# A squared-ReLU MLP as one level of Strassen's scheme, with sums of the up weights made in DRAM

## The chip, the cores and the metric

The kernel runs on one core of a Trainium2 chip. The core has TensorE (PE, with its weight loads listed as PEld), VectorE (DVE), ScalarE (ACT), GpSimd (POOL) and SyncE (SP), each with an instruction queue of its own, and DMA queues that are fed by SP, ACT and POOL. The metric is the device time of one execution in microseconds (us); smaller is better. A profile is one execution recorded by the hardware profiler, and its times count from the start of its span.

## The reference

One decoder layer on x of 512 tokens by 1024. All weights are float32.

```
h = rmsnorm(x, norm_mix_g)
q, k, v, xr, gr, g_attn, g_rnn = split(h @ w_in)            # 1024 x 7168
attn = diff_attention(q, k, v, ...)                         # 8 heads, two softmaxes each, T5 bias, causal
rnn  = gelu(gr) * RG_LRU(causal_conv4(xr))
x = x + (sigmoid(g_attn) * (attn @ w_proj_attn) + sigmoid(g_rnn) * (rnn @ w_proj_rnn)) @ w_out
h2 = rmsnorm(x, norm_mlp_g)
x = x + square(relu(h2 @ w_up)) @ w_down                    # 1024 x 4096, 4096 x 1024
```

The change concerns the last two lines, which are called the MLP here.

## The kernel before

Activations lie transposed, features on the 128 partitions and the 512 tokens along a row. Every float32 product is made of float32r matmuls: `split` (line 129) writes a high part (a cast by ACT) and a low part (source less high part, by DVE) of each operand, and `mm3` (line 124) adds three matmuls into one PSUM bank: high by high, high by low, low by high. So one product of 128 by 128 weights with 512 tokens is three matmuls of 512 columns, recorded as lines 125, 126 and 127. All calls of DVE, ACT and POOL go through one helper that keeps them in program order (recorded as line 66).

Weights come in units of 128 x 1024 float32 (512 KB): four blocks of 128 in the contraction by 256 outputs. The class `Weights` (line 81) loads a unit on SP into `wraw` (two buffers), casts it to `whi` on ACT and subtracts to `wlo` on DVE (four buffers each); `ahead` and `raws` say how many units are cast and loaded before their use. `cols_proj` (line 137) takes units in order and issues for each 24 matmuls of 512 columns into two banks.

The order of work is that of the program text, with generators that interleave stages:

- the input norm and the first gates (0 to about 45 us);
- QKV projections of four head pairs, and attention in 39 steps of which each holds parts of one or more of 32 (head, row block) softmaxes (function `attention`, which keeps a table of what is done at which step). Between the parts of a step, `fill_in` issues pieces of the next pair's projection. The QK norm takes its power on POOL (`rstd_of`, line 203), and DVE applies it two pieces later. POOL also writes and reads back a small table in DRAM for the norm behind attention (lines 579 and 583);
- the recurrent branch in four chunks, interleaved with the remaining gates and the attention projection (`tick`, line 787);
- the recurrent projection (`y_rnn`), then w_out in four blocks (`merged`, line 835), where the residual goes into x2, and x2 scaled by the norm's gain is split into h2T. The sum of squares for the second norm is collected on POOL;
- the MLP (lines 866 to 912) in two chunks of 2048 hidden features. A chunk has eight `cols_proj` over h2T, drained by `relu2` (ReLU and square on ACT, then split), and four over the chunk's 16 hidden blocks, drained by `down`, which multiplies by the second norm's 1/(mean square) and adds to x2 (DVE). The norm can wait because ReLU squared turns a factor on the input into its square on the output. The last block of the last chunk is done in three parts, two of them 256 tokens wide, so that the output leaves early.

Matmuls of 256 columns with one weight load each occur at two places: in the QKV projection, where the activations are the stationary operand, and in the two last parts of the down projection.

## Time and profile before

| | |
|---|---|
| median of 3 runs | 896.83 us (894.88 to 896.98) |
| the profiled execution | 897.49 us, span 895.6 us |
| instructions | 11845, of which 4704 matmuls and 4704 weight loads |
| HBM read, written | 87.89 MB, 4.76 MB |
| mean DMA rate | 101 GB/s |

A row of the timeline is: start in us, duration in us, engine, line, operation, what it writes and reads, shape, and in brackets the idle time before it with what ended it. A row of the groups by line is: line, engine, operation, output and inputs, shape, count, then the busy time of the group and the mean duration of one in ns, then the idle time of the engine just before them and what ended it. A row of a windows view is: the stretch, its length, then busy time and count for each engine asked for (PE alone, or PE, PEld, DVE, ACT and POOL in that order), the granted TensorE clock, the busy share of the DMA engines and GB/s. A row of the DMA queues is: packets, megabytes, and the time of the packets as a share of 16 engines' span; one of the DMA issues: count, KB each, median us to landing. In the list of waits the numbers are total us, times, and the longest. Matmuls overlap, so that the duration of one is longer than its share of the stream.

### The profile page before, as it was taken

Reading aid. Unit: us, or ns where it says so; the run is one execution under the profiler, and the core shown is the slowest. Engines: PE = TensorE matmul, PEld = TensorE weight load, DVE = VectorE, ACT = ScalarE, POOL = GpSimd, SP = SyncE. Lnnn points to the kernel's source line nnn. Section 1 sums busy time; section 2 is a strip of 40 time slices with the busy share of each in tenths; the row PEclk is TensorE's granted clock in tenths of the full one; section 3 lists DMA queues with packets and bytes.
Section 4 is the critical chain, followed back from the end, with each engine's and each line's share of the span. In section 5 each row is a group of like instructions: output and inputs, shape, how many; then the busy total and the mean of one; then the engine's idle time right before and its main releaser. Section 6 shows DMA issues by size and latency. Waiting matters only on the chain.

```text
span 895.6 us, 11845 instructions
## 1 busy us (share of the span) xinstructions
PE 888.7 (99%) x4704; PEld 751.7 (84%) x4704; DVE 497.3 (56%) x874; ACT 397.1 (44%) x643; POOL 63.1 (7%) x64
## 2 busy tenths in 40 slices
PE   9999999999999999999999999999999999999998
PEld 7899999999888777888878888888888888888887
DVE  6765688877865256787677554433233333333331
ACT  6444355455545337657733344555312235552110
POOL 0021212222000000000000031000000000000000
PEclk9999999999999999999999999999999999999999
DMA  6348222221312332332133533233332232223320
GB/s 204 130 135 249 76 59 75 81 61 59 106 60 83 95 131 69 106 107 93 54 111 95 191 110 102 68 123 103 101 98 94 94 94 94 94 94 105 122 103 25
DMA packets 31048, 90.80 MB, mean 101 GB/s; under 512 B 3712, under 2 KB 6728, under 8 KB 30992
## 3 DMA queue, kind: packets, MB, share of 16 engines
q1 hardware_dynamic: 30096, 87.93, 30.5%
q0 software_dynamic: 896, 2.11, 1.1%
q8 instruction: 37, 0.61, 0.3%
q14 instruction: 19, 0.16, 0.1%
HBM read 87.89 MB, written 4.76 MB: 103 GB/s over the span
## 4 chain that ended last, share of the span: by engine, by line
PE 92%; DMA 3%; DVE 2%; ACT 2%; issue 1%; SPq 0%; ACTq 0%
PE acc L125 27%; PE acc L127 27%; PE acc L126 27%; PE at L511 2%; DMA wraw<-in_w_in_dram 2%; PE at L125 2%; PE at L126 2%; PE at L127 2%; ACT whi L66 1%; PE at L545 1%; DVE wlo L66 1%; PE at L463 1%; PE at L576 1%; DMA wraw<-in_w_pa_dram 0%; ACT tt L66 0%
## 5 line engine op out<-in xcount | busy, mean ns | idle before, releaser
L66 DVE TENSOR_TENSOR wlo<-wraw,whi 128x1024 fp32r<-128x1024 f32 (+2 forms) x150 | 177.9, 1198 | 170.9 <-ACT whi L66 170.2
L66 ACT CAST whi<-wraw 128x1024 fp32r<-128x1024 f32 (+2 forms) x150 | 149.8, 1011 | 191.3 <-PE acc L126 140.5
L125 PE MATMUL acc<-whi,hT 128*128 128x256 f32 x384 | 111.4, 290 | 0.0
L126 PE MATMUL acc<-wlo,hT 128*128 128x256 f32 x384 | 108.9, 284 | 0.0
L127 PE MATMUL acc<-whi,hT 128*128 128x256 f32 x384 | 108.8, 283 | 0.0
L127 PE MATMUL acc<-h2T,wlo 128*128 128x512 f32 x256 | 100.5, 393 | 0.0
L125 PE MATMUL acc<-h2T,whi 128*128 128x512 f32 x256 | 100.4, 392 | 0.0
L126 PE MATMUL acc<-h2T,whi 128*128 128x512 f32 x256 | 99.7, 389 | 0.0
L125 PE MATMUL acc<-hT,whi 128*128 128x512 f32 x208 | 82.3, 396 | 0.0
L127 PE MATMUL acc<-hT,wlo 128*128 128x512 f32 x208 | 81.5, 392 | 0.5 <-DVE wlo L66 0.5
L126 PE MATMUL acc<-hT,whi 128*128 128x512 f32 x208 | 81.5, 392 | 0.0
L125 PEld LDWEIGHTS acc<-whi,hT 128*128 128x128 f32 x384 | 73.2, 191 | 4.3 <-issue 3.0
L126 PEld LDWEIGHTS acc<-wlo,hT 128*128 128x128 f32 x384 | 73.3, 191 | 0.7 <-issue 0.5
L127 PEld LDWEIGHTS acc<-whi,hT 128*128 128x128 f32 x384 | 73.2, 191 | 0.6 <-issue 0.4
L66 ACT ACTIVATE pe<-pe,nm 128x128 f32<-128x128 f32 (+3 forms) x64 | 35.5, 556 | 65.3 <-DVE nm L66 65.3
L126 PEld LDWEIGHTS acc<-h2T,whi 128*128 128x128 f32 x256 | 48.1, 188 | 10.9
L127 PEld LDWEIGHTS acc<-h2T,wlo 128*128 128x128 f32 x256 | 48.1, 188 | 10.7
L125 PEld LDWEIGHTS acc<-h2T,whi 128*128 128x128 f32 x256 | 48.1, 188 | 10.0
L66 POOL TENSOR_TENSOR rs<-ms,mhalf 128x8 f32<-128x8 f32 (+1 forms) x25 | 39.7, 1589 | 213.9 <-DVE ms L66 213.9
L125 PE MATMUL acc<-up,whi 128*128 128x512 f32 (+1 forms) x136 | 51.7, 380 | 0.0
L127 PE MATMUL acc<-up,wlo 128*128 128x512 f32 (+1 forms) x136 | 51.6, 379 | 0.0
L125 PE MATMUL acc<-upT,whi 128*128 128x512 f32 (+1 forms) x136 | 51.4, 378 | 0.0
(197 smaller groups left out, 1662.5 us busy)
## 6 DMA issues: line engine op xcount, KB each, us to landing
wraw<-in_w_in_dram SPq DMA_DIRECT2D x52, 512.0 KB, 3.4
wraw<-in_w_up_dram SPq DMA_DIRECT2D x32, 512.0 KB, 3.3
wraw<-in_w_dn_dram SPq DMA_DIRECT2D x32, 512.0 KB, 3.3
wraw<-in_w_pa_dram SPq DMA_DIRECT2D x8, 512.0 KB, 4.4
wraw<-in_w_pr_dram SPq DMA_DIRECT2D x8, 512.0 KB, 3.3
wraw<-in_w_o_dram SPq DMA_DIRECT2D x8, 512.0 KB, 4.4
trep<-tdram SPq DMA_DIRECT2D x8, 320.0 KB, 5.0
toep<-trep SPq DMA_DIRECT2D x8, 256.0 KB, 3.9
```

Source lines behind the costliest of these rows:

```text
L66: ins = f(*a, **k)
L125: T.matmul(o, l[0], r[0], start=first, stop=False)
L126: T.matmul(o, l[0], r[1], start=False, stop=False)
L127: T.matmul(o, l[1], r[0], start=False, stop=last)
L463: T.transpose(out=ps[:, t * P:(t + 1) * P], in_=qn[t // 2][:, c0:c0 + P], identity=ident)
L511: T.matmul(lg[c][:, :N], qT[r, x0, i * P:(i + 1) * P], kT[r, y0, :N], start=a == 0, stop=a == 2)
L545: T.transpose(out=tp[:, b * P:(b + 1) * P], in_=st[s][:, b * P:(b + 1) * P], identity=ident)
L576: T.matmul(ps[:, t:t + 1], sq[:, t * P:(t + 1) * P], ones, start=True, stop=True)
```

## The change

The MLP is divided into 16 units: for each of four chunks of 1024 hidden features two up units (512 outputs by 1024 contraction) and two down units (512 outputs by 1024 contraction). A unit is a 2 x 2 by 2 x 2 block product over half outputs, half contraction and half tokens, and is made of seven products M1 to M7 instead of eight. Each product is 8 blocks of weights with 256 tokens, three matmuls each: 24 matmuls of 256 columns. Three PSUM banks (X, Y, Z) serve a unit; several products add into the same bank one after the other.

The seven products need sums and differences:

- of the activations: for the up units from h2 (made once in `merged`, seven forms in `h2s`), for the down units from the squared ReLU (made in `up_out`, with `act_sums` on DVE, seven forms in `us`);
- of the down weights: made in place in the raw buffers by DVE, four additions of 128 x 1024 a unit (`plus_for`);
- of the up weights: made in DRAM. `weight_sums` copies blocks with two transfers a unit on ACT's queue, and adds with three accumulating transfers on POOL's queue. `prep` advances it, by half a transfer for each attention step, then in `tick` and in later stages. SP loads the sums like other weights, with seven loads for an up unit and four for a down unit.

The order of the products, the casts ahead of them (up to four units of weights) and the moments of the deferred ACT and DVE work (`later`, in multiples of `STEP`, counted in planned time) are written out. The first up units are begun with three of four blocks of the contraction. The norm is applied differently: x2 is multiplied by the mean square, and the regions that the last two units write are multiplied by its reciprocal at the end. The squares are added by DVE instead of POOL. The host lays w_up and w_down out in blocks for this.

```diff
-    for ch in range(2):
-        for j in range(8):
-            wb.cols(w_up, 2048 * ch + 256 * j)
-        for j in range(4):
-            wb.cols(w_dn, 256 * j, 16 * ch, 16)
+
+    DU = [(kind, ch, m) for ch in range(4) for kind in ("up", "down") for m in range(2)]
+    UP = [v for v in range(16) if DU[v][0] == "up"]
+    sums13, sums42 = ({v: dp.tile([2, P, 1024], F32, name=f"t{z}{v}", tag=f"t{z}{v}") for v in UP} for z in "ab")
+
+    def blocks(v):
+        kind, ch, m = DU[v]
+        return (w_up if kind == "up" else w_dn)[2 * ch + m].rearrange("a b p c -> (a b) p c")
+
+    def weight_sums():
+        def init(v):
+            A.dma_start(sums13[v], blocks(v)[0:4:3])
+            A.dma_start(sums42[v], blocks(v)[2:4])
+
+        init(UP[0])
+        for n in range(10):
+            if n + 1 < 8:
+                init(UP[n + 1])
+            if n < 8:
+                G.dma_start(sums13[UP[n]], blocks(UP[n])[1:2].broadcast_to([2, P, 1024]), accum_op=ALU.add, max_dma_last_dim=8192)
+                yield
+            if 0 <= n - 1 < 8:
+                G.dma_start(sums42[UP[n - 1]][1], sums13[UP[n - 1]][0], accum_op=ALU.add, max_dma_last_dim=8192)
+                yield
+            if 0 <= n - 2:
+                G.dma_start(sums42[UP[n - 2]][0], sums42[UP[n - 2]][1], accum_op=ALU.add, max_dma_last_dim=8192)
+                yield
+
+    ws_gen, ws_owed = weight_sums(), [0.0]
+
+    def prep(amount):
+        ws_owed[0] += amount
+        while ws_owed[0] >= 1.0:
+            ws_owed[0] -= 1.0
+            next(ws_gen, None)
...
+            prep(0.5)
...
+            prep(0.08 * cost)
...
-        run(y_rnn(mh))
+        mh = hp.tile([P, 2, KT, S], F32R, tag="hT", name="mT")
+        mh = [mh[:, j] for j in range(2)]
+        for _ in y_rnn(mh):
+            prep(0.15)
...
+    FORM = {"M1": 0, "M4": 1, "M2": 2, "M5": 3, "M6": 4, "M7": 5, "M3": 6}
+
+    def hi_part(dst, src):
+        A.copy(dst[:, 0], src)
+
+    def lo_part(dst, src):
+        V.tensor_tensor(out=dst[:, 1], in0=src, in1=dst[:, 0].bitcast(F32), op=ALU.subtract)
+
+    def act_sums(f, fs, which=range(4)):
+        for n in which:
+            a, b = {0: (f[1], f[2]), 1: (fs[:, 0], f[0]), 2: (f[0], f[1]), 3: (f[3], fs[:, 1])}[n]
+            V.tensor_tensor(out=fs[:, n], in0=a, in1=b, op=ALU.add if n == 3 else ALU.subtract)
...
+            f1 = scratch[:, 4 + 2 * (j % 2):6 + 2 * (j % 2), :].rearrange("p a (u s) -> p a u s", u=2)
+            d = h2s[j // 2][:, :, :, j % 2, :]
+            f = f1[:, 0, 1, :], f1[:, 0, 0, :], f1[:, 1, 0, :], f1[:, 1, 1, :]
             for c in range(2):
                 t = 2 * j + c
                 V.tensor_tensor(out=x2[:, t, :], in0=ps[c], in1=x2[:, t, :], op=ALU.add)
-                split(h2T[0][:, t, :], h2T[1][:, t, :], x2[:, t, :], smt[:, C_G2 + t:C_G2 + t + 1])
+                g2 = smt[:, C_G2 + t:C_G2 + t + 1]
+                if c == 0:
+                    for h in range(2):
+                        A.activation(f[h], x2[:, t, 256 * h:256 * h + 256], AF.Copy, scale=g2)
+                else:
+                    A.activation(f1[:, 1, ::-1, :], x2[:, t, :].rearrange("p (h s) -> p h s", h=2), AF.Copy, scale=g2)
+            fs = fin.tile([P, 4, 2, 256], F32, tag="fs", name="h2fs")[:, :, 0, :]
+            for src, dst in ((f[0], d[:, :, 0]), (f1[:, 1], d[:, :, 1:3])):
+                hi_part(dst, src)
+            act_sums(f, fs)
+            for src, dst in ((f[0], d[:, :, 0]), (f1[:, 1], d[:, :, 1:3])):
+                lo_part(dst, src)
+            hi_part(d[:, :, 3:7], fs)
+            lo_part(d[:, :, 3:7], fs)
             for c in range(2):
                 t = 2 * j + c
-                sq = ssq if t == 0 else fin.tile([P, S], F32, tag="relu", name="sq2", bufs=2)
+                sq = ssq if t == 0 else scratch[:, 2 + t % 2, :]
                 A.activation(sq, x2[:, t, :], AF.Square)
                 if t:
-                    G.tensor_tensor(out=ssq, in0=ssq, in1=sq, op=ALU.add)
+                    owing.append(lambda sq=sq: V.tensor_tensor(out=ssq, in0=ssq, in1=sq, op=ALU.add))
...
+    ORD = {"up0": ("M1", "M2", "M6", "M5", "M7", "M3", "M4"), "up1": ("M1", "M5", "M6", "M2a", "M7", "M2b", "M4", "M3"),
+           "down0": ("M1", "M5", "M6", "M2", "M7", "M3", "M4"), "down1": ("M1", "M5", "M6", "M2", "M7", "M3", "M4")}
...
+    steps = []
+    for v, (kind, ch, m) in enumerate(DU):
+        if v == 0:
+            g, r = range(3), range(3, 4)
+            steps += [step(0, "M1", g), step(0, "M2", g), step(0, "M5", g), step(1, "M1", g), step(0, "M1", r), step(0, "M2", r), step(1, "M1", r)]
+            steps += [step(0, p, r if p == "M5" else every) for p in ("M6", "M5", "M7", "M3", "M4")]
+        else:
+            steps += [step(v, p) for p in ORD[kind + str(m)] if (v, p) != (1, "M1")]
...
+    for v, p in ops:
+        up, b = DU[v][0] == "up", blocks(v)
+        if up:
+            need.append(len(loads) + 1)
+            loads.append((v, p, {"M1": b[0], "M2": b[2], "M3": b[3], "M5": sums13[v][0], "M7": sums13[v][1], "M6": sums42[v][1], "M4": sums42[v][0]}[p]))
+        else:
+            for q, n in (("M1", 0), ("T", 1), ("M3", 3), ("M2", 2)):
+                if p == "M1":
+                    loads.append((v, q, b[n]))
+            need.append(None)
...
+    def load():
+        while n_load[0] < len(loads) and n_load[0] < n_free[0] + 4:
+            n = n_load[0]
+            if n < EARLY or len(wb.raw) == len(wb.reqs):
+                v, p, src = loads[n]
+                t = fin.tile([P, 4, 256], F32, tag="rx", name="raw", bufs=2) if n % 4 < 2 else wp.tile([P, 4, 256], F32, tag="wraw", name="raw", bufs=2)
+                nc.sync.dma_start(t, src.rearrange("p (k c) -> p k c", k=4))
+                raw[v, p] = t
+                n_load[0] += 1
+            else:
+                break
+
+    def drop(v, p):
+        dead.add((v, p))
+        while n_free[0] < n_load[0] and loads[n_free[0]][:2] in dead:
+            n_free[0] += 1
...
+    def plus_for(n):
+        if n >= len(ops) or n in added or not loaded(n):
+            return
+        added.add(n)
+        v, p = ops[n]
+        if DU[v][0] == "down":
+            for q, x, y in (("M5", "M1", "T"), ("M6", "M1", "M3"), ("M7", "T", "M3"), ("M4", "M2", "M1")):
+                if q == p:
+                    V.tensor_tensor(out=raw[v, x], in0=raw[v, x], in1=raw[v, y], op=ALU.add)
+                    if q == "M4":
+                        drop(v, "M1")
+
+    def cast_lo():
+        hi, lo, src, (v, p) = half.pop(0)
+        V.tensor_tensor(out=lo, in0=src, in1=hi.bitcast(F32), op=ALU.subtract)
+        lows[0] += 1
+        if DU[v][0] == "up":
+            drop(v, p)
+        elif p in ("M7", "M3", "M4"):
+            drop(v, {"M7": "T", "M3": "M3", "M4": "M2"}[p])
+        load()
+
+    def cast_hi():
+        n = len(units)
+        v, p = ops[n]
+        plus_for(n)
+        slots[0] -= 1
+        src = raw[v, p if DU[v][0] == "up" else {"M5": "M1", "M6": "M1", "M7": "T", "M4": "M2"}.get(p, p)]
+        hi, lo = (wp.tile([P, 4, 256], F32R, tag=t, name=t, bufs=4) for t in ("whi", "wlo"))
+        A.copy(hi, src)
+        units.append((hi, lo))
+        half.append((hi, lo, src, (v, p)))
+
+    def next_lo():
+        if half:
+            cast_lo()
+            plus_for(len(units))
...
+    def up_out(v, p, X, Y, Z):
+        m = DU[v][2]
+        if p == "M1":
+            acts[v] = {"a11": fin.tile([P, 2, 256], F32, tag="a11", name="a11", bufs=2)}
+            us[m] = hp.tile([P, 2, 7, 2, 256], F32R, tag="hT", name="us0") if m == 0 else fin.tile([P, 2, 7, 2, 256], F32R, tag="us", name="us1")
...
+        if p == "M1":
+            A.copy(f0, Y)
+        elif p == "M2":
+            V.tensor_tensor(out=f0, in0=X, in1=f0, op=ALU.add)
+            later(1.1 * STEP if m == 0 else 0.0, lambda: relu2(f0))
+            hl(0, f0, *((1.1, 2.1) if m == 0 else (0.0, 0.6)))
+        elif p == "M6":
+            A.copy(a12, Y)
+        elif p == "M5":
+            A.copy(a22, Z)
+        elif p == "M7":
+            V.tensor_tensor(out=a22, in0=a22, in1=Y, op=ALU.subtract)
+            if m == 1:
+                later(0.0, lambda: relu2(a22))
+                hl(1, a22, 0.6, 1.6)
...
+        elif p == "M4":
+            A.activation(a21, Y, AF.Relu)
+            A.activation(a21, a21, AF.Square)
+            fs = fss[v] = fin.tile([P, 4, 2, 256], F32, tag="fs", name="fs")
+            if m == 0:
+                later(0.0, lambda: relu2(a12))
+                hl(2, a12, 0.5, 1.2)
+                later(1.1 * STEP, lambda: act_sums((f0, a21, a22, a12), fs))
+                hl(slice(3, 7), fs, 2.1, 3.1)
...
+    def down_out(v, p, X, Y, Z):
+        ch, m = DU[v][1:]
+        part = lambda c, h: x2[:, 4 * m + 2 * c:4 * m + 2 * c + 2, 256 * h:256 * h + 256]
+        for q, ps, c, h, op in (("M1", Y, 0, 0, ALU.add), ("M2", X, 0, 0, ALU.add), ("M6", Y, 1, 0, None), ("M5", Z, 1, 1, ALU.add),
+                                ("M7", Y, 1, 1, None), ("M3", Z, 1, 0, ALU.add), ("M4", Y, 0, 1, ALU.add)):
+            if q == p:
+                o = part(c, h)
+                if op is None:
+                    V.tensor_tensor(out=o, in0=o, in1=ps, op=ALU.subtract)
+                else:
+                    V.tensor_tensor(out=o, in0=ps, in1=o, op=op)
+                if ch == 3 and p in ("M2", "M7", "M3", "M4"):
+                    s = slice(256 * h, 256 * h + 256)
+                    V.tensor_tensor(out=o, in0=o, in1=r2[:, s].rearrange("p (o s) -> p o s", o=1).broadcast_to([P, 2, 256]), op=ALU.mult)
+                    t = 4 * m + 2 * c
+                    nc.sync.dma_start(out[t * P:(t + 2) * P, s].rearrange("(u p) s -> p u s", p=P), o)
...
+    def norm2():
+        s2 = fin.tile([P, 2, S], F32R, tag="fs", name="s2")
+        split(s2[:, 0], s2[:, 1], ssq)
         ps = psum("acc")
-        T.matmul(ps, onesr, s2[0], start=True, stop=False)
-        T.matmul(ps, onesr, s2[1], start=False, stop=True)
-        V.tensor_scalar(out=r2, in0=ps, scalar1=1.0 / DM, scalar2=EPS, op0=ALU.mult, op1=ALU.add)
-        V.reciprocal(r2, r2)
+        T.matmul(ps, onesr, s2[:, 0], start=True, stop=False)
+        T.matmul(ps, onesr, s2[:, 1], start=False, stop=True)
+        m = r2
+        V.tensor_scalar(out=m, in0=ps, scalar1=1.0 / DM, scalar2=EPS, op0=ALU.mult, op1=ALU.add)
+        later(32.0, lambda: V.reciprocal(r2, m))
+        for t in range(KT):
+            later(2.0 + 2.5 * t, lambda t=t: V.tensor_tensor(out=x2[:, t, :], in0=x2[:, t, :], in1=m, op=ALU.mult))
...
+    seen, banks = {}, {}
+    for s, (v, p, pairs, halves) in enumerate(steps):
+        kind, ch, m = DU[v]
+        if v not in banks:
+            banks[v] = [psum("acc") for _ in range(3)]
+        X, Y, Z = banks[v]
+        b = {"M2": X, "M5": Z, "M3": Z}.get(p, Y)
+        src = h2s if kind == "up" else us
+        for _ in range(2):
+            if len(units) < number[v, p] + 4 and can_cast():
+                next_lo()
+                cast_hi()
+        while lows[0] <= number[v, p]:
+            if half:
+                next_lo()
+            else:
+                assert can_cast()
+                cast_hi()
+        hi, lo = units[number[v, p]]
+        f = FORM[p]
+        k = seen.get((v, p), 0)
+        seen[v, p] = k + len(pairs) * len(halves)
+        for u in halves:
+            for n, i in enumerate(pairs):
+                a = src[i // 2]
+                for e, (l, r) in enumerate(((hi, 0), (hi, 1), (lo, 0))):
+                    T.matmul(b[:, 256 * u:256 * u + 256], l[:, i, P * u:P * u + P], a[:, r, f, i % 2],
+                             start=p in ("M1", "M2", "M5") and k == n == u == e == 0, stop=i == 3 and e == 2, skip_group_check=True)
+        if seen[v, p] == 8:
+            finish((v, p))
+            (up_out if kind == "up" else down_out)(v, p, two(X), two(Y), two(Z))
+        tick(STEP * len(pairs) * len(halves) / 8)
+        next_lo()
+        if s == 9:
+            norm2()
+        prep(0.4)
...
+    up4 = g["w_up"][0].reshape(4, 2, P, 8, 2, 256).transpose(3, 1, 4, 2, 0, 5).reshape(8, 2, 2, P, 1024)
+    dn4 = g["w_down"][0].reshape(4, 2, 2, 2, P, 2, 2, 256).transpose(0, 5, 2, 6, 4, 1, 3, 7).reshape(8, 2, 2, P, 1024)
```

143 lines of the change are left out of this document (85 added, 58 removed).

## The prediction

> **What bounds the kernel now.** I read the engines' busy table and the chain of waits first, to see which engine sets the end, then the MLP by windows and by timeline, then the groups by line inside the MLP, the waits, and the DMA views.
>
> ```profile
> PE 888.7 (99%) x4704; PEld 751.7 (84%) x4704; DVE 497.3 (56%) x874; ACT 397.1 (44%) x643; POOL 63.1 (7%) x64
> PE 92%; DMA 3%; DVE 2%; ACT 2%; issue 1%; SPq 0%; ACTq 0%
> ```
>
> TensorE has work in 99% of the span and carries 92% of the chain that ended last. A busy TensorE need not be a fast one, so the rate is read from starts. The first two rows are stretches of the MLP (up with the first down; the last down chunks), the next two are the first and the last of 96 matmuls of 256 columns with which the down projection ends.
>
> ```profile
> 540.00:804.00 264.00, 264.00 (x1156) 1.00 0.30 96
> 880.40:891.80 11.40, 11.40 (x97) 1.00 0.10 36
> ...
> 880.45 0.28 PE L125 MATMUL acc<-up,whi 128*128 128x256 f32 x1
> ...
> 891.75 0.28 PE L127 MATMUL acc<-upT,wlo 128*128 128x256 f32 x1
> ```
>
> A 512-column matmul takes 264.0 / 1156 = 0.2284 us of the stream; a 256-column one (891.75 - 880.45) / 95 = 0.119 us. Both run at granted clock 1.00, no gap is left, and the DMA engines are 30% busy. So the MLP, from 540 to 892, is bound by the number of matmul columns and by nothing else. DVE and ACT in the same stretch (540 to 892) have little to do:
>
> ```profile
> L66 DVE TENSOR_TENSOR wlo<-wraw,whi 128x1024 fp32r<-128x1024 f32 x61 | 75.3, 1237 | 99.7 <-ACT whi L66 99.7
> L66 ACT CAST whi<-wraw 128x1024 fp32r<-128x1024 f32 x61 | 64.1, 1051 | 139.9 <-PE acc L126 139.9
> L66 ACT ACTIVATE rsq<-relu 128x512 f32<-128x512 f32 x32 | 20.2, 632 | 1.4 <-PE acc L858 0.4
> L66 ACT ACTIVATE relu<-acc 128x512 f32<-128x512 f32 x32 | 19.0, 595 | 63.8 <-PE acc L127 63.8
> L66 ACT CAST up<-rsq 128x512 fp32r<-128x512 f32 x16 | 9.9, 621 | 0.5
> ```
>
> **The change part by part.** *Matmuls.* Today the MLP issues 1488 matmuls of 512 columns and 96 of 256: 1488 x 0.2284 + 96 x 0.119 = 351.3 us. After it, 16 units of 7 products of 24 matmuls of 256 columns: 2688 x 0.119 = 319.9 us. One eighth of the columns goes, 43.9 us, but a column costs 0.465 ns in a 256-wide matmul instead of 0.446, which gives 12.5 us back: **-31.4 us**. The 96 rows are the operation itself (weights stationary, activations moving, one load for each matmul). The ends of the range are 11.40 / 97 = 0.1175 us (315.9, -35.4) and 6.00 / 49 = 0.1224 (329.0, -22.3) from a stretch of the QKV projection below; I take 0.119, from starts, because the edges of a window cut matmuls and the projection has its operands the other way round.
>
> ```profile
> 57.50:63.50 6.00, 6.00 (x49) 1.00 0.59 197
> ```
>
> [...]
>
> *DVE.* It now holds the sums and differences that the scheme needs. How close its instructions follow one another, from starts:
>
> ```profile
> 39.44 0.74 DVE L66 SCALAR_TENSOR_TENSOR hT<-xT,smt,hT 128x512 fp32r<-128x512 f32 x1
> 40.10 1.22 DVE L66 TENSOR_TENSOR wlo<-wraw,whi 128x1024 fp32r<-128x1024 f32 x1
> 41.24 0.68 DVE L66 TENSOR_TENSOR xT<-xT,rb 128x512 f32<-128x512 f32 x1
> 41.84 0.74 DVE L66 SCALAR_TENSOR_TENSOR hT<-xT,smt,hT 128x512 fp32r<-128x512 f32 x1
> ...
> L66 DVE RECIPROCAL r<-r 128x512 f32<-128x512 f32 x1 | 3.4, 3353 | 0.0
> ```
>
> 1.14 us for 1024 elements and 0.60 for 512, so about 2.2 for 2048. A down unit has 7 low parts (8.0), 4 sums of raw weights (4.6) and 7 drains of PSUM into x2 (4.2): 16.8 us in the 20.0 us that its 7 x 24 matmuls take (84%). An up unit has 7 low parts (8.0), 3 drains (1.8), 4 sums of activations (2.4) and low parts of 7 forms (three of 512, one of 2048: 4.0): 16.2 us (81%). The two units that write the output have four more multiplications each, 19.2 us of 20.0. The norm, moved among them, adds the reciprocal and nine or ten passes of 512, about 9.5 us once. In all 8 x 16.8 + 8 x 16.2 + 4.8 + 9.5 = 278 us of 320: it fits, as the rows of a unit add up, but DVE goes from a spare engine to one that is 87% full. *ACT* in an up unit, by the durations above: 7 high parts (7.4), 4 pairs of relu and square (4.9), 3 copies and 3 casts of 512 (3.7), a cast of 2048 (2.1): 18.1 us of 20.0; in a down unit 7.4.
>
> The stalls that this leaves cannot be seen in the trace of before. The place for them is a down unit's start. Its four raw weights stay until the last product's weights are summed, so the next unit's first load waits for them: a load, a high part and a low part are 3.3 + 1.05 + 1.24 = 5.6 us (the rows of a load stand below), against 2.86 us for a product, with up to four units cast ahead (8.6 us) as cover. From both sides: 0 if the cover holds, 8 x (5.6 - 2.86) = 22 us if it never does. I take 1 us for each of the 8 down units, **+8 us**, nearer the lower end since the cover is longer than the chain; a gain below nothing is excluded, as TensorE has no idle time to give.
>
> *Start and end of the MLP.* The last merged block must be added, scaled, summed and split before its part of the contraction is used. In the queue of DVE that is two additions (1.2), four sums of 256 (1.7 by the row below), low parts of 256, 512 and 1024 (2.2), with ACT's casts between them (2 to 3) and two or three low parts of weights (1.14 each): 9 to 11 us. The first four steps, that use three of the four blocks, cover 72 x 0.119 = 8.6 us. 0 to 4 us, I take **+2**. The same work for the three blocks before, with the adding of the squares that leaves POOL, is about 8 us of DVE for each, beside the 48 x 0.2284 = 11 us of a block's matmuls: nothing, while that cover of 3 us stands. At the end the last addition and multiplication have 512 elements instead of 256, one after the other: **+0.5 us**.
>
> ```profile
> L66 POOL TENSOR_TENSOR ssq<-ssq,sq 128x512 f32<-128x512 f32 x7 | 12.2, 1750 | 42.5 <-ACT sq L66 42.3
> ...
> 892.07 0.42 DVE L66 TENSOR_TENSOR y<-acc,r 128x256 f32<-128x256 f32 x1 [4.82 <-PE acc L127]
> 892.53 0.42 DVE L66 TENSOR_TENSOR x<-y,x 128x256 f32<-128x256 f32 x1
> ```
>
> *The sums in DRAM.* For each of 8 up units ACT issues two copies of 1 MB and POOL three accumulating transfers (1 MB, 0.5, 0.5), 24 on POOL. From the end of attention step 1 one of these is due at every second step; 19 by the last step, the other five in the recurrent stage.
>
> ```profile
> q1 hardware_dynamic: 30096, 87.93, 30.5%
> wraw<-in_w_in_dram SPq DMA_DIRECT2D x52, 512.0 KB, 3.4
> trep<-tdram SPq DMA_DIRECT2D x8, 320.0 KB, 5.0
> L66 POOL DMA_DIRECT2D rb<-rdram x8 | 4.4, 555 | 12.2 <-PE at L463 4.0 <-ACT whi L66 2.3 <-ACT pe L66 2.1
> 0.75 0.39 SPq L283
> ```
>
> SP's own queue gets 88 loads in the MLP instead of 64. In an up unit that is 7 x 0.52 MB in 20 us, 184 GB/s of the 322 that 16 engines give by the rate below; it stays covered while the four raw buffers hold, and SP's loads of sums wait for transfers issued over 100 us before.
>
> The issues are small: 16 x 0.39 = 6.2 us on ACT, 24 x 0.56 = 13 us on POOL, both spread over 250 us on engines that are 44% and 7% busy, so nothing on the path. The transfers move, by queue 1, 87.93 MB / (0.305 x 16 x 895.6 us) = 20.1 GB/s on each DMA engine. Spread over 16 engines, a copy of 1 MB (1.05e6 bytes) takes 3.3 us and an accumulation, if it costs a copy and a second read, 6.5 us at most. In attention, loads run ahead by two raw buffers and two cast units and absorb that. In the recurrent stage they do not:
>
> ```profile
> 300.00:343.00 43.00, 42.47 (x183) 33.83 (x181) 21.27 (x26) 16.63 (x22) 0.00 (x0) 1.00 0.41 134
> ...
> 313.94 3.36 DMA wraw<-in_w_in_dram
> ...
> 317.39 1.06 ACT whi L66
> ...
> 318.48 1.24 DVE wlo L66
> ...
> 319.73 3.32 DMA wraw<-in_w_in_dram
> ```
>
> Load, high part and low part follow one another without slack here (5.8 us from load to load; 24 x 0.2284 = 5.5 us of matmuls), and five or six accumulations fall into this stage and the one behind it. Each can hold one load back by up to its own 3 us: 0 to 15 us, I take **+4**, as only three fall before 343.
>
> **Sum**, against the profiled run of 897.49 us (span 895.6 and 1.9 around it): -31.4 + 8 + 2 + 0.5 + 4 = -16.9, 880.6 us. That run is 0.7 above the median of 896.83, so the forecast for the median is **880 us**. Its own range, with the matmul at 0.1175 to 0.1224 and the stalls at 0 to 15 in all or twice that: 866 to 891. A difference under 0.3% (2.7 us) can hardly be told from none here.
>
> **The rivals.** *POOL waits in attention and everything behind it is late (slower, 33%).* The first accumulation needs the first copy, issued in the same breath, and POOL takes its instructions in order: in the waits below it sits until a DMA has landed. Behind that wait stand the powers of the QK norm, for which DVE, in order too, waits in turn.
>
> ```profile
> POOL rb L66 <- DMA rdram<-rs: 1.9, 1, 1.9
> ...
> 86.62 0.56 PE at L511 x6
> ...
> 136.39 0.55 PE at L511 x6
> ...
> 101.48 2.62 POOL L66 TENSOR_TENSOR rs<-ms,mhalf 128x8 f32<-128x8 f32 x1 [11.52 <-DVE ms L66]
> ...
> 108.03 0.68 DVE L66 TENSOR_TENSOR qn<-acc,rs 128x512 f32<-128x512 f32 x1
> ```
>
> The two rows of L511 are the logits of steps 1 and 9. The power is done at 104.1 and used at 108.0; started late by over 4 us it holds DVE up. What decides is the number of DMA engines that a transfer with two blocks as its outer dimension gets. With 16 the first copy, issued near 90, is in by 96. With two it takes 1.05e6 / (2 x 20.1e3) = 26 us, the second, queued behind it, 52, and an accumulation 26 to 52 more: POOL's second would start at 142, the fifth, that needs the second's result, at 168 to 194, where its turn (step 9) is about 140. Less some 6 us of slack that is 22 to 48 us late; I price it at 25, near the lower end, because 20.1 GB/s is the rate of packets that share an engine with others. 880 + 25 = **905 us**, 893 to 920 by the delays. For it: the copy and the wait stand side by side in the code. Against it: 320 KB from DRAM to DRAM land in 5.0 us above, and nothing in this trace tells of a transfer on few engines. It turns slower than before from a delay of 17 us on.
>
> The Trainium skill (DMA: Bandwidth & Descriptors, Rules for kernel authors) speaks for this rival: a transfer is split along its slowest dimension that is not 1, so that an outer count of 2, a broadcast of two copies too, is confined to two of the 16 engines. No run here shows it yet.
>
> *The vector engines become the bound (15%).* DVE, at 84 to 96%, answers in order: a drain that stands behind a late low part holds a PSUM bank that is reused two products later. If a down unit costs DVE's sum and one chain of 5.6 us in turn (22.4, and 24.8 for the last two), the MLP takes 8 x 20.0 + 6 x 22.4 + 2 x 24.8 = 344 us instead of 328: **896 us**, 890 to 902. For it the 96% of the last two units, against it the cover of four units.
>
> *The gain is larger (5%):* no stall and no collision, 897.5 - 31.4 + 0.5 - 0.7 = **866 us**. That the change does not do what it says, the sums being late for the MLP, is no case: the last accumulation is issued near 380, the first up weights are loaded after 520.
>
> **How the numbers follow.** 47% for the forecast (all of it faster by over 0.3%, but for one point on each side). The wait on POOL: 5 of its 33% faster, 5 the same, 23 slower. The vector bound: 11 faster, 2 the same, 2 slower. The larger gain: 5. Together 0.47 - 0.02 + 0.05 + 0.11 + 0.05 = 0.66 faster, 0.08 the same, 0.26 slower. Below 866 lie some 4%, above 907 about 15%, so 866 to 907 holds 8 in 10.
>
> **What would show it.** Right: the MLP at 320 to 332 us with 2688 matmuls of 256 columns 0.119 us apart, DVE near 87% in it, no long wait of POOL for a DMA, attention from 80 to 300 as before. The rival on POOL: its waits for the copies of 20 us and more before 200, idle TensorE there, and a recurrent stage that starts 20 to 45 us late. The vector bound: TensorE idle at each down unit's start, released by a low part. I would be wrong altogether if the 256-column matmul came at 0.13 us or more, since 2688 x 0.13 = 349 us is what the MLP takes now.

## The result, and the profile after

The changed kernel takes **1202.34 us** (median of 4 runs, 1201.75 to 1203.4) against 896.83: 1.3415 times as long, interval 1.3391 to 1.3438. The forecast was 880, with 866 to 907 as its range. It was wrong in sign and by 322 us.

The page of the profile after: engines, the granted clock in 40 slices, and the chain that ended last.

```profile
PE 912.4 (76%) x5808; PEld 818.6 (68%) x5808; DVE 668.0 (56%) x1084; ACT 474.8 (40%) x739; POOL 76.7 (6%) x80
PEclk9997675859876796857699999999989989989989
PE 45%; DMA 28%; DVE 9%; issue 8%; ACT 8%; POOL 1%; SPq 0%; ACTq 0%; POOLq 0%; DVEq 0%
```

TensorE went from 99% of the span to 76%, and from 92% of the chain to 45%; transfers have 28% of it. The clock row says where: it is at 5 to 8 in most slices from the fourth to the twentieth, 30 us each, all of them ahead of the MLP. The windows view, cut at the stages (attention, its end and the recurrent stage in the first three rows, then the two projections, then the MLP):

```profile
80.00:300.00 220.00, 114.42 (x822) 105.43 (x821) 75.75 (x223) 48.89 (x115) 30.15 (x24) 0.73 0.38 108
300.00:500.00 200.00, 124.18 (x745) 105.12 (x743) 80.04 (x224) 56.89 (x130) 27.78 (x27) 0.81 0.42 107
500.00:726.40 226.40, 164.06 (x668) 131.03 (x669) 102.23 (x137) 93.08 (x127) 8.49 (x10) 0.84 0.34 88
726.40:820.50 94.10, 93.43 (x409) 76.33 (x408) 67.86 (x95) 40.16 (x57) 0.00 (x0) 1.00 0.39 129
820.50:1195.50 375.00, 338.28 (x2691) 331.67 (x2689) 288.65 (x323) 194.37 (x246) 0.00 (x0) 0.95 0.38 122
```

Attention and the MLP before, in the same view:

```profile
80.00:300.00 220.00, 220.00 (x1609) 197.26 (x1608) 158.99 (x450) 109.06 (x251) 40.34 (x36) 1.00 0.26 79
...
539.70:892.00 352.30, 352.30 (x1587) 291.14 (x1585) 124.69 (x132) 123.09 (x162) 3.65 (x2) 1.00 0.29 95
```

The MLP begins at 820.5 instead of 539.7: 281 us are lost before it. It then lasts 375 us where it lasted 352.3: 23 us lost, where 21 were to be gained (-31.4 + 8 + 2 + 0.5). These are two different losses. In the first three rows after TensorE is busy for 403 of 646 us, and the DMA engines are only 34 to 42% busy: something waits for transfers that do not fill the engines. The chain in order of time names them (start, length, what):

```profile
88.79 22.17 DMA ta<-in_w_up_dram
...
113.50 29.38 DMA wraw<-in_w_in_dram
...
148.43 56.48 issue
...
212.75 47.69 DMA rb<-rdram
...
299.25 32.12 DMA rdram<-rs
```

The first is a copy of 1 MB into the sums: 22.2 us. The second is an ordinary load of weights; the median of such loads is 7.2 us here and was 3.4. To the third the chain gives no cause; its end, 204.9, is the end of a wait of POOL in the next view. The last two are the small table of row sums that attention writes to DRAM and reads back: 256 KB (the table spread over all partitions) in 47.7 us, and 2 KB in 32.1. POOL's timeline shows how it came to this.

```profile
111.27 1.59 POOL L66 DMA_DIRECT2D ta<-in_w_up_dram  x1 [21.62 <-DMA ta<-in_w_up_dram]
116.88 2.64 POOL L66 TENSOR_TENSOR rs<-ms,mhalf 128x8 f32<-128x8 f32 x1 [4.02 <-DVE ms L66]
139.35 1.45 POOL L66 DMA_DIRECT2D ta<-in_w_up_dram  x1 [19.84 <-DMA ta<-in_w_up_dram]
...
204.92 0.87 POOL L66 DMA_DIRECT2D tb<-ta  x1 [56.49 <-DMA ta<-in_w_up_dram]
205.55 1.95 POOL L66 TENSOR_TENSOR rs<-ms,mhalf 128x8 f32<-128x8 f32 x1
...
299.25 0.65 POOL L66 DMA_DIRECT2D rdram<-rs  x1 [0.30 <-POOL rs L66]
299.89 0.86 POOL L66 DMA_DIRECT2D tb<-ta  x1
```

Three times by 205 us POOL stands in front of an accumulation until a transfer has landed (21.6, 19.8 and 56.5 us), and the power that follows in its queue, which the QK norm needs, is issued behind that. The list of waits (total, times, longest) adds the rest: who waits for small transfers and loads, and that ScalarE stood too.

```profile
DVE of L66 <- DMA rb<-rdram: 126.0, 5, 37.9
ACT whi L66 <- DMA wraw<-in_w_in_dram: 125.7, 22, 24.8
...
POOL tb L66 <- DMA ta<-in_w_up_dram: 104.1, 2, 56.5
...
POOL rb L66 <- DMA rdram<-rs: 66.7, 4, 31.6
...
POOL ta L66 <- DMA ta<-in_w_up_dram: 41.5, 2, 21.6
...
ACT pt L66 <- DMA ta<-in_w_up_dram: 22.4, 1, 22.4
```

The last row is the beginning of the chain: ScalarE, which issues the copies, issued those of the next unit only when the first copy had landed, and stood idle for 22.4 us. In the run with wide transfers below it issues the same four copies within 2.7 us. Why it could not here is not shown.

In the MLP, the matmuls come as forecast and the stalls do not. Four units of the second chunk, in order up, up, down, down, in the windows view (columns as above):

```profile
921.20:941.00 19.80, 19.80 (x171) 19.80 (x170) 12.69 (x15) 12.40 (x17) 0.00 (x0) 1.00 0.62 206
941.00:960.80 19.80, 19.80 (x171) 19.80 (x170) 13.68 (x15) 14.78 (x20) 0.00 (x0) 1.00 0.49 160
960.80:991.70 30.90, 23.71 (x170) 22.77 (x169) 25.05 (x29) 12.69 (x16) 0.00 (x0) 0.89 0.23 69
991.70:1012.10 20.40, 20.24 (x170) 20.07 (x169) 16.72 (x18) 8.21 (x9) 0.00 (x0) 1.00 0.36 119
```

A unit without a stall is 168 matmuls in 19.8 us, 0.118 us each. But the first down unit of a chunk takes 30.9 us, and the same unit of the other chunks 34.3, 31.5 and 31.8 (from starts of its matmuls): 49 us over four times 19.8. In it DVE has 25.05 us of work, more than 19.8, and in the other three 12.7 to 16.7.

### The profile page after: what moved, and what is told of

It reads as the page before. It is cut to its first block, busy times and chain, and to the rows that moved or that the text cites. A ratio compares the mean times of both kernels' runs of the same rounds, so it can differ in the third digit from the quotient of the medians.

```text
span 1199.9 us, 14488 instructions
## 1 busy us (share of the span) xinstructions
PE 912.4 (76%) x5808; PEld 818.6 (68%) x5808; DVE 668.0 (56%) x1084; ACT 474.8 (40%) x739; POOL 76.7 (6%) x80
## 4 chain that ended last, share of the span: by engine, by line
PE 45%; DMA 28%; DVE 9%; issue 8%; ACT 8%; POOL 1%; SPq 0%; ACTq 0%; POOLq 0%; DVEq 0%
PE acc L1169 20%; DMA rb<-rdram 12%; DMA wraw<-in_w_in_dram 8%; PE acc L125 8%; PE acc L127 8%; PE acc L126 8%; DMA rdram<-rs 6%; DVE wlo L66 3%; ACT whi L66 3%; DMA ta<-in_w_up_dram 2%; ACT a L66 2%; DVE raw L66 1%; POOL rs L66 1%; DMA wraw<-in_w_pa_dram 1%; DVE x L66 1%
## 5 line engine op out<-in xcount | busy, mean ns | idle before, releaser
L1169 PE MATMUL acc<-us,whi 128*128 128x256 f32 x896 | 174.4, 296 | 21.7 <-ACT whi L66 13.0
L1169 PEld LDWEIGHTS acc<-us,whi 128*128 128x128 f32 x896 | 147.6, 202 | 25.6 <-ACT whi L66 14.3
L66 ACT CAST whi<-raw 128x1024 fp32r<-128x1024 f32 x112 | 114.7, 1048 | 116.3 <-DVE raw L66 96.4
L1169 PE MATMUL acc<-h2s,whi 128*128 128x256 f32 x896 | 158.7, 280 | 1.1 <-ACT whi L66 0.6
L66 DVE TENSOR_TENSOR wlo<-raw,whi 128x1024 fp32r<-128x1024 f32 x112 | 135.3, 1219 | 33.0 <-ACT whi L66 33.0
L66 ACT CAST whi<-wraw 128x1024 fp32r<-128x1024 f32 (+2 forms) x86 | 82.7, 982 | 149.2 <-DMA wraw<-in_w_in_dram 125.7
L1169 PEld LDWEIGHTS acc<-h2s,whi 128*128 128x128 f32 x896 | 136.5, 187 | 2.1 <-ACT whi L66 1.0
L1169 PE MATMUL acc<-us,wlo 128*128 128x256 f32 x448 | 129.9, 294 | 10.4 <-DVE wlo L66 10.4
L1169 PE MATMUL acc<-h2s,wlo 128*128 128x256 f32 x448 | 124.7, 280 | 3.3 <-DVE wlo L66 3.3
L125 PE MATMUL acc<-hT,whi 128*128 128x512 f32 x208 | 86.1, 414 | 32.7 <-ACT whi L66 26.2
L1169 PEld LDWEIGHTS acc<-us,wlo 128*128 128x128 f32 x448 | 89.0, 200 | 11.5 <-DVE wlo L66 11.5
L1169 PEld LDWEIGHTS acc<-h2s,wlo 128*128 128x128 f32 x448 | 84.0, 188 | 3.9 <-DVE wlo L66 3.7
## 6 DMA issues: line engine op xcount, KB each, us to landing
ta<-in_w_up_dram POOLq DMA_DIRECT2D x8, 1024.0 KB, 51.3
tb<-ta POOLq DMA_DIRECT2D x8, 512.0 KB, 32.8
```

The lines of the kernel that those rows point to most:

```text
L66: ins = f(*a, **k)
L125: T.matmul(o, l[0], r[0], start=first, stop=False)
L1169: T.matmul(b[:, 256 * u:256 * u + 256], l[:, i, P * u:P * u + P], a[:, r, f, i % 2], start=p in ("M1", "M2", "M5") and k == n == u == e == ...
```

## The experiments

**The shape of the transfers.** Theory: the copies and accumulations have two blocks as their outermost dimension, and that makes them slow. Rival: they cost what they move, or what they wait for, in any shape. Where no range stands beside a time it is that of one run; the kernel before took 896.4 to 897.8 beside these.

Both kinds wide, the 128 rows outermost on both sides. Only the transfers into `sums13` are changed; the copy into `sums42`, whose two blocks lie next to one another on both sides, keeps its two blocks outermost, and the accumulations of 512 KB had 128 rows outermost from the start:

```diff
-A.dma_start(sums13[v], blocks(v)[0:4:3])
+A.dma_start(sums13[v].rearrange("a p c -> p a c"), blocks(v)[0:4:3].rearrange("a p c -> p a c"))
-G.dma_start(sums13[UP[n]], blocks(UP[n])[1:2].broadcast_to([2, P, 1024]), ...)
+G.dma_start(sums13[UP[n]].rearrange(...), blocks(UP[n])[1:2].broadcast_to([2, P, 1024]).rearrange(...), ...)
```

> Theory A: the copies and the accumulations into sums13 have an outer dimension of 2 and so run on two DMA engines; what waits behind them makes the loss before the MLP (attention 80 to 500 us instead of 80 to 300, recurrent stage 226 us instead of 145). With the 128 rows outermost a copy of 1 MB lands in about 6 us and an accumulation in about 8; attention is back at 80 to about 305, the recurrent stage at 145 to 155, the MLP stays at 375: about 917 to 930 us. Rival B: 32 MB of copies and accumulations are too much in any shape, or an accumulation waits long whatever its shape: above 1100 us, with accumulations still landing after 30 us or more.

Measured: 972.37 us (1.0862 of before, 1.0829 to 1.0895), MLP from 589.7. The lines of the DMA issues (count, KB, median us to landing), after and in this run:

```profile
wraw<-in_w_in_dram SPq DMA_DIRECT2D x52, 512.0 KB, 7.2
...
ta<-in_w_up_dram POOLq DMA_DIRECT2D x8, 1024.0 KB, 51.3
...
tb<-ta POOLq DMA_DIRECT2D x8, 512.0 KB, 32.8
```

```profile
wraw<-in_w_in_dram SPq DMA_DIRECT2D x52, 512.0 KB, 3.6
...
ta<-in_w_up_dram ACTq DMA_DIRECT2D x8, 1024.0 KB, 7.1
...
ta<-in_w_up_dram POOLq DMA_DIRECT2D x8, 1024.0 KB, 13.8
...
tb<-ta POOLq DMA_DIRECT2D x8, 512.0 KB, 8.2
```

The same bytes, accumulated in 13.8 us instead of 51.3, and SP's loads back from 7.2 to 3.6: 230 of the 305 us are the shape. The last row, 512 KB, fell from 32.8 to 8.2 us though its own shape is the same: it had stood behind the narrow ones. The direction was as expected, the size was not: 51 us still go before the MLP.

The records of the single pieces of a transfer show what the shape does. In the changed kernel the first copy into `sums13` is 16 pieces of 64 KB, and two of them are under way at a time, 2.4 us each, from 90.3 to 110.5. The copy into `sums42` issued behind it has 14 of its 16 pieces under way at once from 92 on, beside those two. Narrow, an accumulation into `sums13` is 128 pieces of 8 KB, 0.63 us each; two pieces of this size are under way in 240 of the 390 us in which any is. Wide, it is 256 pieces of 4 KB, 0.33 us each, and nine or more are under way in 61 of 80 us. Per piece the bytes in a us stay about the same, so what changed is how many pieces are under way.

One kind at a time, only the copies wide (first) and only the accumulations wide (second):

> The copies on ACT's queue get 128 rows outermost, the accumulations on POOL's queue stay on two engines. If it is POOL's queue that matters (an accumulation of 40 us or more, with the small transfers of the attention norm in the same queue behind it), most of the loss stays: 1050 to 1150 us. If it is the copies in 64 KB pieces that hold up the weight loads and POOL's first waits, most of it goes: under 1000 us.

> The reverse: accumulations with 128 rows outermost, copies still on two engines. If POOL's queue matters, most of the loss goes: two waits of about 20 us at the start and slower weight loads are left, 940 to 990 us. If the copies matter, 1050 us or more.

Measured: 1170.29, MLP from 788.5, most of the loss left as POOL's queue would have it, and 20 us more than its range; and 1067.08, MLP from 685.7, the branch in which the copies matter. Against no transfers at all (538.7, below) the start of the MLP is late by 282 us with both narrow, 250 with narrow accumulations, 147 with narrow copies, 51 with both wide. The two do not add up: either kind alone, if narrow, costs a large part of the whole, and neither is the cause alone.

The shape kept, but the small transfers of the row sums on SP instead of POOL's queue:

```diff
-G.dma_start(rdram[h, :].rearrange("(p t) -> p t", p=P), rs)
+nc.sync.dma_start(rdram[h, :].rearrange("(p t) -> p t", p=P), rs)
```

(and the same for the way back)

> The changed kernel (1202.34 us) with one edit: attention's small row-sum transfers (row sums to DRAM and back) are issued from SP in place of POOL, so they no longer share a queue with the narrow accumulations; transfers and their pace stay. Theory (queue order): most of the loss is these small transfers standing behind the accumulations and POOL standing behind its own waits; 1000 to 1070. Rival (slow transfers hold SP's loads and the DMA engines whoever shares the queue): 1130 to 1200.

Measured: 1134.85. The theory that the shared queue is most of it fell: 67 of 305 us. The narrow transfers delay SP's loads (13.9 us in the median) and POOL itself (it waits 151.7 us for copies and accumulations into `sums13`) without it.

**Without the sums.** The up units load plain blocks, nothing is copied or accumulated:

```diff
-next(ws_gen, None)
...
-"M5": sums13[v][0], "M7": sums13[v][1], "M6": sums42[v][1], "M4": sums42[v][0]
+"M5": b[0], "M7": b[1], "M6": b[1], "M4": b[2]
```

> The kernel leaves out the sums of the up weights altogether (raw blocks are loaded in their place), with all else as in the changed kernel. Both theories: attention and the recurrent stage as before the change (MLP begins at 540 us), and the MLP's own loss alone is left: 375 us in it, about 916 us in all. If the MLP comes out near 330 us instead, its stalls came from the loads of the sums or from what the transfers left behind, and not from the order of ACT and DVE.

Measured: 921.07. The stages ahead of the MLP are those of before (it starts at 538.7), and the MLP lasts 376 us, its first down units 32.6, 31.7, 32.1 and 32.3. So the second loss is there without the first, and belongs to the MLP's own work.

**Where the last 51 us go.** Wide, the copy into `sums42` too, with the copies on POOL's queue (off ScalarE) and the row sums on SP:

> Wide transfers (972.37 us), with the copies issued from POOL in place of ScalarE, and attention's small row-sum transfers moved from POOL's queue to SP's. Theory: of the 51 us that the wide form still loses before the MLP, most comes from SP's loads being held behind ScalarE's copies, and from the small transfers on POOL; then the MLP starts at 545 to 560 and the kernel takes 925 to 945. Rival (the transfers take DMA time from the loads wherever they are queued, at 0.71 of the engines busy): MLP at 575 to 595 and 955 to 980.

Measured: 946.54, MLP from 565.5: 24 us of the 51 came back, a little less than the theory had. Which of the moves gave it was not separated. Next, nothing issued in attention at all (`prep(0.5)` removed there), on the same queues:

> Wide transfers, copies issued from POOL, and none of the sums issued during attention: the first units' in the recurrent stage and the projections behind it, the others during the MLP itself. Theory: attention is undisturbed (first recurrent projection at 445 as before the change), there is room for the transfers later, and the MLP starts at 540 to 550 and takes its 375: 915 to 930. Rival (the loss only moves): the recurrent stage or the MLP's weight loads lose as much as attention did, 950 to 980.

Measured: 982.40, MLP from 598.7. The rival, and worse: the loss moved and grew. Then the sums in 32 small steps, 0.3 of a step for each one of attention and 0.02 instead of 0.08 in the recurrent stage:

> Wide transfers, all of the sums' transfers on POOL's queue, the small row-sum transfers on SP's, and the sums spread evenly from attention to the MLP in 32 steps of at most 2 MB (in the two earlier forms they came within 220 or 145 us, at 0.80 and 1.03 of the DMA engines). Theory (only bursts cost): the MLP starts at 540 to 552 and the kernel takes 918 to 935. Rival (each transfer costs the same wherever it stands): the MLP starts at 562 or later, 943 or more.

Measured: 959.00, MLP from 576.6. And with 0.4 in attention and none in the recurrent stage:

> As the paced form (959.00 us), but none of the sums' transfers is issued in the recurrent stage: 0.4 of a step in attention (there the paced form ran at 0.53 of the DMA engines and PE stayed busy in the whole 220 us), none from 300 to 500, the rest later. Theory (only the burst at 300 to 345, where the engines stood at 1.02, cost the paced form its 37 us): the MLP starts at 538 to 546 and the kernel takes 917 to 926. Rival (the sums cost the recurrent stage's start or the stages after it wherever they stand): MLP at 555 or later, 935 or more.

Measured: 959.37, MLP from 577.1. The rates in the program had no effect behind attention, and the traces say why. The windows of the run with nothing in attention, then of the last one:

```profile
300.00:445.00 145.00, 107.99 (x401) 82.06 (x400) 57.82 (x74) 49.25 (x66) 29.13 (x35) 0.86 1.03 287
```

```profile
80.00:270.00 190.00, 190.00 (x1456) 172.32 (x1455) 143.61 (x416) 96.05 (x226) 42.67 (x34) 1.00 0.63 157
...
300.00:345.00 45.00, 31.35 (x105) 23.36 (x104) 7.68 (x7) 6.74 (x8) 8.48 (x10) 0.77 1.03 278
```

In attention POOL has powers to compute, which hold its queue to TensorE's pace: at 0.63 of the DMA engines TensorE is busy for 190 of 190 us. Behind attention POOL has nothing left but transfers. It issued the rest as fast as they landed, the engines went to 1.03, and the recurrent stage's loads waited. So POOL was given something to wait for (the gated form):

```diff
+def pace():            # before each step of the sums from the 17th on
+    ...
+    A.copy(a, smt[:, :1])
+    G.tensor_copy(g, a)
```

> As the paced form, with 15 steps of the sums in attention, and from the 17th on each step waits on POOL for one element that ScalarE copies at that place of its own queue (some 16 copies of 128x1, a few us at most in all): in the forms before, POOL had nothing to wait for behind attention and issued all that was left at once. Theory (only the burst at 300 to 345, at 1.02 of the DMA engines, cost the 37 us): the MLP starts at 538 to 548, and the kernel takes 918 to 930. Rival (the sums cost the recurrent stage the same spread out): 555 or later, 935 or more.

Measured: 936.33, MLP from 549.2.

```profile
80.00:300.00 220.00, 220.00 (x1611) 197.13 (x1611) 159.21 (x450) 109.29 (x251) 49.10 (x41) 1.00 0.63 159
300.00:345.00 45.00, 40.11 (x170) 32.24 (x169) 17.15 (x19) 13.53 (x17) 0.00 (x0) 0.96 0.52 150
...
500.00:556.00 56.00, 51.28 (x232) 42.22 (x231) 36.02 (x57) 27.97 (x50) 14.30 (x17) 0.97 0.90 263
```

The start is 1.2 us past its expectation, and the time 6 us, which puts it inside the rival's range. But the burst at 300 to 345 is gone, and with it 28 us of the start, so most of the loss was the burst. What remains ahead of the MLP stands at 300 to 345 (4.9 us of TensorE idle) and at 500 to 556 (4.7 us, the engines at 0.90). Wide and spread, the sums cost 10.5 us ahead of the MLP instead of 282, and 15 in all (936.33 against 921.07); of the other 5, 3 are in the first up unit, 26.2 us instead of 22.9.

**Why the first down unit takes 32 us.** All these runs have the kernel without the sums in DRAM (921.07) as their base. Theory of order: DVE and ScalarE work in order, and activation work stands ahead of the weights' parts. Rival: there is simply more work than time. The timelines of DVE and ScalarE in the changed kernel, at the start of that unit:

```profile
968.13 1.22 DVE L66 TENSOR_TENSOR raw<-raw 128x1024 f32<-128x1024 f32 x1
969.27 0.68 DVE L66 TENSOR_TENSOR a<-acc,a 128x512 f32<-128x512 f32 x1
973.25 1.23 DVE L66 TENSOR_TENSOR us<-fs,us 128x1024 fp32r<-128x1024 f32 x1 [3.30 <-ACT us L66]
974.39 1.22 DVE L66 TENSOR_TENSOR wlo<-raw,whi 128x1024 fp32r<-128x1024 f32 x1
```

```profile
969.38 1.04 ACT L66 CAST whi<-raw 128x1024 fp32r<-128x1024 f32 x1 [3.71 <-DVE raw L66]
...
972.18 1.04 ACT L66 CAST us<-fs 128x1024 fp32r<-128x1024 f32 x1
```

ScalarE waits 3.7 us for DVE's sum of raw weights, works off the activations, and then DVE waits 3.3 us for ScalarE's cast of a form: each in turn is idle for the other, and TensorE waits for both. Of its 7.2 idle us in this unit, 3.0 end with a low part of weights, 1.9 with a high part, 1.5 with DVE's addition into x2 and 0.8 with a low part of an activation. Three orders were tried. DVE's low part ahead of the drains (`next_lo()` moved in front of `up_out`/`down_out`):

> As the kernel without the sums (921.07 us; the up units load their raw blocks, so the products that need a sum are formed with a plain block), and the low part of the next weight unit is taken on DVE before the work on the finished product, not behind it. Theory (order): the first down unit of each chunk stalls because DVE's queue has activation work ahead of the low part that TensorE waits for; then these four units fall from 32 us to 21 to 25 and the kernel takes 880 to 895. Rival (throughput): DVE and ScalarE simply have more work in that unit than TensorE, whatever the order: the units stay at 30 to 33 and the time at 912 to 925.

Measured: 936.62, the unit at 34 to 37.5 us, worse than either had it. The products' order, the first half of M1, M5, M2 ahead:

```diff
+steps += [step(v, p, g) for g in (range(2), range(2, 4)) for p in ("M1", "M5", "M2")] + [step(v, "M6")]
```

> As the kernel without the sums of the up weights (921.07 us, up products formed with plain blocks), and the first down unit of each chunk begins with the halves of M1, M5 and M2 that read the first up unit's outputs, so that some 4 us of matmuls do not wait for the second up unit's forms, and M2 (no sum) stands ahead of M6. Theory (a chain: form of the second up unit, raw sum, cast, low part, one after the other on ScalarE and DVE): the first down unit falls from 32 us to 23 to 28, the kernel takes 885 to 907. Rival (DVE and ScalarE need that long for their work in any order): 31 to 33, 915 to 925.

Measured: 924.04, 31 to 33 us. ScalarE's cast of the next weights ahead of the activation work (`next_lo()` and `cast_hi()` in front of `tick`):

> As the kernel without the sums of the up weights (921.07 us, up products formed with plain blocks), and ScalarE casts the next weight unit as soon as a product is finished, ahead of the activation work of that step, in place of behind it. In the trace DVE idles 3 us twice at the first down unit of each chunk, each time for a cast that stands behind activation work on ScalarE. Theory (the order of ScalarE's queue): the first down unit falls from 32 us to 22 to 27, 890 to 908. Rival (DVE's own work, 23 of these 32 us, and the sums on it set the end): 915 to 930.

Measured: 918.28, 30.5 to 36 us. None of the three orders is it. Then work was left out. The four sums of raw weights of a down unit:

```diff
-V.tensor_tensor(out=raw[v, x], in0=raw[v, x], in1=raw[v, y], op=ALU.add)
```

> As the kernel without the sums, and the down units' four DVE additions of raw blocks are left out as well, so M5, M6, M7 and M4 of the down units use plain blocks. Theory (chain): in a down unit one product needs DVE's sum, then ScalarE's cast, then DVE's low part, one after the other with activation work between; without the sum the first down unit of a chunk falls from 32 us to 20 to 24 and the kernel takes 878 to 895. Rival (activation work is the load): 1.2 us less for each of 64 additions on an engine that is not the bound gives 905 to 920.

Measured: 902.66, the unit at 27.0 to 29.1 us, between the two expectations. (The kernel has 32 of these additions, four in each of eight down units, not the 64 of the rival.) And, with the sums kept, the second up unit's four forms:

```diff
-later(0.3 * STEP, lambda: act_sums((f0, a21, a22, None), fs, (0, 1, 2)))
-hl(3, fs[:, 0], 0.4, 0.5)
-hl(slice(4, 6), fs[:, 1:3], 1.1, 1.2)
```

(and the fourth form likewise)

> As the kernel without the sums of the up weights (921.07 us, up products formed with plain blocks), and the second up unit's four differences of activations, their casts and low parts are left out as well (5.4 us of DVE and 2.3 us of ScalarE in each chunk, right where the first down unit begins; its products take the plain forms in their place). Theory (DVE has more to do around the start of the first down unit than TensorE has there, whatever the order): the unit falls from 32 us to 23 to 27, and the kernel takes 890 to 906. Rival (the down units' chain of sum, cast and low part alone sets the end): 29 to 32, 912 to 922.

Measured: 890.84, the unit at 22.5 in three chunks and 27.1 in the first, about as the theory had it. The unit in the second chunk, without the raw sums and then without the forms:

```profile
674.80:701.80 27.00, 22.32 (x171) 21.70 (x170) 20.18 (x25) 12.70 (x16) 0.00 (x0) 0.94 0.26 79
```

```profile
673.40:695.90 22.50, 20.75 (x170) 20.14 (x170) 19.82 (x22) 10.04 (x13) 0.00 (x0) 1.00 0.30 95
```

DVE has about the same work in both, 20.2 and 19.8 us. Yet one takes 27.0 and the other 22.5, so DVE's sum is not all of it: the forms, which pass from DVE to ScalarE and back, cost more than the raw sums of about equal DVE time. ScalarE also has 2.7 us less to do in the second (10.0 by 12.7); whether that or the passing costs more was not separated. An order of the two queues that hides this was not found.

Half of the raw sums (M7, M4) on POOL, which is idle in the MLP:

```diff
+if p == "M6":
+    G.tensor_tensor(out=raw[v, "T"], in0=raw[v, "T"], in1=raw[v, "M3"], op=ALU.add)
...
```

(and the sum for M4 likewise)

> As the kernel without the sums of the up weights (921.07 us, up products formed with plain blocks), and of the down units' four additions of raw blocks two (for M7 and M4) are made on POOL ahead of time, in place of DVE. Theory (DVE has too much to do around the first down unit): 2.4 us less DVE work in each down unit, the first down unit of a chunk falls from 32 us to 25 to 28, and the kernel takes 900 to 910; the form without any of the four sums (902.66) is the bound. Rival (POOL's addition takes about twice the 1.75 us of its 128x512 row, and the products wait for that): 921 or more.

Measured: 928.80, slower, as in the rival's range but not for its reason. Timelines of POOL and DVE:

```profile
684.91 2.64 POOL L66 TENSOR_TENSOR raw<-raw 128x1024 f32<-128x1024 f32 x1 [51.47 <-DVE raw L66]
```

```profile
685.21 2.88 DVE L66 TENSOR_TENSOR us<-a,us 128x512 fp32r<-128x512 f32 x1
688.02 0.68 DVE L66 TENSOR_TENSOR fs<-a,a 128x512 f32<-128x512 f32 x1
```

POOL's addition itself takes 2.64 us, less than the 3.5 that the rival had it take. But DVE's 512 elements beside it take 2.88 us instead of 0.68: DVE loses most of what it was relieved of.

**Together.** Nothing left out, paced sums and POOL's additions; then paced sums and the split down unit, the latter in several rounds:

> Nothing is left out: the wide and evenly paced sums of the up weights, all issued before the MLP, and the down units' sums for M7 and M4 on POOL. If both edits do what their theories say, MLP start at 540 to 555 and an MLP of about 360: 903 to 920, near the kernel before (896.4) but not under it, since the MLP alone would still take more than the 352 of before. Rival (POOL's additions collide with the transfers it issues or with DVE): 930 or more.

> Nothing is left out: wide transfers, sums issued in attention and behind the recurrent stage, and the split first down unit. If both theories hold, the MLP starts at 538 to 546 and takes 340 to 360: 883 to 910, about the kernel before (896.8). If the chain theory falls, 915 to 926; if the pacing theory falls, 920 or more.

Measured: 963.30; and 952.22 (945.52 to 957.66), 1.0597 of before (1.0533 to 1.0662). Both have the burst behind attention (MLP from 575.3 and 574.3), so they say little of the MLP's edits, whose units are no shorter there (31.0 to 33.8 us). The best complete form is the gated one, 936.33: slower than the kernel before, one run of each, by 38.5 us, 10 of them ahead of the MLP, the rest in it. No version beat the kernel before.

## Why the prediction was wrong, point by point

- **Matmuls, -31.4: right.** 16 units of 19.8 us where no stall is, 316.8 us, or 0.118 for each of 2688 matmuls; 0.119 was forecast. That is -34.5.
- **The sums in DRAM, +4: the step that failed most; +281.** The failing sentence is "Spread over 16 engines, a copy of 1 MB (1.05e6 bytes) takes 3.3 us and an accumulation ... 6.5 us at most". The first copy took 22.2 us, and accumulations 51.3 in the median. Two pieces of the first copy were under way at a time, not 16. Made wide, transfers took 7.1 (copies) and 13.8 us: the ratio of two was right, and the times were still twice the forecast. Nor did the loads "absorb that" in attention: ScalarE's casts waited 125.7 us for weight loads, and even the wide form began the MLP 51 us late, by the burst and the queues for the most part, since 10.5 are left in the gated one. The issues, "nothing on the path", were on it at the start, where ScalarE stood for 22.4 us. The 320 KB in 5.0 us that I held against the rival said nothing of a transfer in two blocks.
- **The rival on POOL, +25 at 33%: right in kind, priced at a tenth.** Its 26 us for a copy on two engines stands beside 22.2 measured, and its waits are in the rows. The Trainium skill's rule (DMA: Bandwidth & Descriptors, Rules for kernel authors: a small outermost count confines a transfer to at most that many engines) agrees with the two pieces at a time and with 51.3 against 13.8 us. The second copy of a unit, which the rival had on two engines as well, had 14 pieces under way at once. And I took one delay of 22 to 48 us, once. The whole list of waits has six of POOL for copies and accumulations (153 us), and the slow transfers held others besides: five waits of DVE for the table read back (126.0) and 22 of ScalarE for loads (125.7). These overlap and are not a sum. A delay that recurs is priced by its count.
- **Stalls at the down units, +8 (0 to 22): mis-sized; +49 in the first down units, about +2 in the others.** I looked for them in the load of raw weights; most of them came from forms and sums (without the forms the unit falls to 22.5 in three chunks, without the sums to 27 to 29). My sum for DVE was right (278 us forecast, 288.65 measured; 66.0 for a chunk's four units, 68.1 measured). It failed at "An up unit has ... low parts of 7 forms": the second up unit's forms can only be made when its last products are done, and fall into the first down unit. So the chunk's 68.1 us lie at 12.7, 13.7, 25.1 and 16.7, and an average of 87% hid one unit at 127% of 19.8. "The vector engines become the bound" was the right rival for the MLP, with 2.4 us a unit where 12 were lost in every fourth.
- **Start, +2: +6.4** (the first two up units at 22.8 and 23.2 us, by 19.8). **The end, +0.5:** not told apart from the 1 us that the span gained behind the last matmul.
- The sum as measured: -34.5 + 281 + 49 + 2 + 6.4 + 1 = 304.9, against 304.3 between the spans (1199.9 - 895.6).

## What to carry to other kernels

Before work is moved to DMA, read off the shape which dimension is outermost on both sides, and price the transfer as if that count were its number of engines (two blocks that lie next to one another on both sides did not count as two here); then multiply the delay by how often an engine's queue stands behind it. Check the balance of an engine for the stretch in which its work becomes possible, not for the average over the stage. A queue that waits for nothing is not paced by where its instructions stand in the program.
